# Three of eight weight pairs by seven products in the last projection's second half, with its row sums, a split affine step and a later halving of the last bank

## The chip, the cores and the metric

The kernel runs on one core of one Trainium2 chip. The metric is the device time of one execution in microseconds, the median over runs. A profile of one execution comes with it.

## The reference

The reference is one hybrid decoder layer on 256 tokens of width 2048, in float32: an input projection, two attention branches, a merge and an output projection with a layer norm, a gated MLP (width 5632) with a second layer norm, and a per-layer embedding at the end. What the change touches is the last line:

```python
x = layer_norm(ALPHA * x + ffn, ln2_g[i], ln2_b[i])
x = x + jax.nn.sigmoid(x @ w_ple_gate[i]) * (p[i] @ w_ple_proj[i])
```

The product x @ w_ple_gate is 256 x 2048 by 2048 x 2048. It is the last matrix product of the kernel, and everything that follows it is exposed.

## The kernel before, in words

**Splitting.** TensorE multiplies in a rounded float32 format (F32R). To keep the precision, each operand is split into a high part and a low remainder, and a product is the sum of three: high x high, high x low, low x high. Weights come in 284 units of 128 x 2048 floats. For each, SP issues two loads of 512 KB into `raw` (four buffers), ScalarE copies each into `hi` (line 231), and VectorE subtracts to get `lo` (line 236). `hi` and `lo` have six buffers each, which hold three units. The function `prep` (line 210) does that, and `unit` (line 254) calls it for a unit two or three places ahead of the one that TensorE takes.

**Plain pairs.** In the stages that compute token-major outputs, `x_half` (line 395) goes through the contraction in pairs of 128-row steps; a unit holds the weights of one pair for 1024 output columns. Two token halves (t) and two halves of the columns (c) make four PSUM banks of 512 columns. `x_mm` (line 340, its matmul on line 353) issues, for each of the two steps of a pair, 2 token halves x 3 products x 2 column halves: 24 matmuls of 512 columns a pair.

**Pairs by seven products.** A pair is also a 2 x 2 block product (two token halves, two contraction steps), and Strassen's scheme with seven products in place of eight does it with 21 matmuls (`seven`, line 356, its matmuls on line 373). It needs combinations of the weights (`combine_all`, line 144, computes them early on VectorE, lines 149 and 152, and stores them in DRAM as `tfd`, line 154), which `prep_seven` (line 161) later loads as `full` and splits into `ts` (line 179). It also needs sums of the activations (`x_sums`, line 376), split in the same way. Three of the seven products go straight into three of the four banks; the other four gather in four extra banks `ms`, and behind the last such pair a function `joined` adds those on VectorE into the four outputs. The gv, wo and dn stages work so for some of their pairs. The list of pairs is GVW, WOW or DNW.

**The last stage.** The gate product is done in two halves of 1024 columns, pg0 and pg1 (units 268 to 275 and 276 to 283), of eight pairs each. pg0 starts beside the second layer norm; pg1 keeps its last two pairs as a tail (`tail=2`), which is gone through bank by bank, so that the evacuation of one bank runs beside the matmuls of the next. With `fine=True` pg1's last bank (t = 1, c = 1) is kept in two halves of 256 columns, `pg1_11` and `pg1_11b`, for the whole of its sum, so that the very last evacuation is short. The evacuation `ev_o` (lines 1539 to 1551) is tanh on ScalarE (line 1545), two operations on VectorE (1546, 1548) and a store.

**What runs beside it.** The generator `affine` (line 1182, its operation on line 1187) multiplies the normalized `z2` by the gain and adds the bias, in sixteen steps of 128 x 512 on VectorE. `pull(n)` takes n steps of such generators behind each pair; in pg0 it is three a pair.

**What sets the order.** The queue of SP, which issues the loads, is in program order. The other engines' orders are chosen by a scheduler that places what is ready, the earlier in the program first. `keep_in_program_order` pins an instruction behind the one written last before it on the same engine; each step of `affine` is pinned so. The pool S8 has 15 tiles of 128 x 2048 floats: in the gate/up loop (`for n in range(NF)`, line 1371) it holds the four tiles of x1T, up to ten of hT, and the tiles of combinations.

Of the kernel before, what the change touches and what calls it, by code (L numbers as in the profile page):

```python
# [9 lines left out]
F32 = mybir.dt.float32  # L10
# [38 lines left out]
GV0 = 32  # L49
GVW = (1, 2, 4, 5)  # L50
WOW = ((1, 2, 4, 5), ())
WOP = tuple(sorted(set(WOW[0] + WOW[1])))
COMBW = range(14, 23)
COMB0 = 13
# [12 lines left out]
def tile_block(ctx: ExitStack, tc: tile.TileContext, wu, xw, wfv, wpp, xT_in, x_in, pT_in, wlr,  # L67
# [70 lines left out]
    tsi = {u: j for j, u in enumerate(units7)}  # L138
    tsd = dr.tile([len(units7), P, 1024], F32, name="tsd")
    units7w = [GV0 + i for i in GVW] + [WO0 + nh * 8 + i for nh in range(2) for i in WOW[nh]]  # L140
    tsw = {u: j for j, u in enumerate(units7w)}
    tfd = dr.tile([len(units7w), P, 2048], F32, name="tfd")

# [12 lines left out]
    def combs_gen(us):  # L156
        for u in us:
            yield from combine_all(u)
            yield
# [94 lines left out]
    def unit(ahead=3):  # L254
        u = n_used[0]
        n_used[0] += 1
        while n_prep[0] < min(NU, u + ahead):
            prep()
        return ready.pop(u)
# [77 lines left out]
        else:  # L337
            nc.vector.scalar_tensor_tensor(o, a, scale, tmp, ALU.mult, ALU.add)

    def x_mm(banks, w, a, toks, first, last, cs=(0, 1), part=None):  # L340


        hi, lo = w
        for t in toks:
            ah = a[:, t * P:t * P + P]
            al = a[:, 256 + t * P:256 + t * P + P]
            for i, (x, v) in enumerate(((ah, hi), (ah, lo), (al, hi))):
                for c in cs:
                    bs = banks[t][c]
                    m = 512 // len(bs)  # L350
                    for j in range(len(bs)) if part is None else (part,):
                        o = c * 512 + j * m
                        nc.tensor.matmul(bs[j][:, 0:m], lhsT=x, rhs=v[:, o:o + m],  # L353
                                         start=first and i == 0, stop=last and i == 2)

    def seven(banks, ms, w, act, kt, first, last):

# [35 lines left out]
                    mixers.pop(0)  # L393

    def x_half(name, act, K, evac, pulls=0, head=0, tail=0, mid=None, done=None, end=None,
               fine=False, ws=(), joined=None, begin=None, lean=False):


        ms = []
        banks = [[[mmtile(f"{name}_{t}{c}")] for c in range(2)] for t in range(2)]  # L400
        if fine:
            banks[1][1].append(mxtile(f"{name}_11b"))
        n = K // 2

        def mm(i, w, toks, cs=(0, 1), part=None):
            for j in range(2):
                kt = 2 * i + j
                x_mm(banks, (w[0][j], w[1][j]), act[kt // 4][:, kt % 4, :], toks,
                     kt == 0, kt == K - 1, cs, part)

        us = [unit(2) for _ in range(head)]
        if begin is not None:
            begin(lambda i, t: mm(i, us[i], (t,)))
        for i in range(head, n - tail):
            if i in ws:
                if i == ws[0]:
                    ms.extend(mmtile(f"{name}m{j}") if j % 2 == 0 else mxtile(f"{name}m{j}")
                              for j in range(4))
                seven(banks, ms, unit(), act, 2 * i, i == ws[0], i == ws[-1])
                if i == ws[-1]:  # L420
                    joined(ms)
            else:
                mm(i, unit(), (0, 1))
            pull(pulls)
            if mid is not None and i in mid:
                mid[i]()
        us = [unit(3 - (i if lean else 0)) for i in range(tail)]

        def tail_mm(t, c, i, put=True):
            mm(n - tail + i, us[i], (t,), (c,))  # L430
            if not put:
                return lambda: evac(t, c, banks[t][c][0])
            if i == tail - 1:
                evac(t, c, banks[t][c][0])

        if end is not None:
            end(tail_mm)
            return
        for t in range(2):
            for c in range(2):  # L440
                bs = banks[t][c]
                for j, ps in enumerate(bs):
                    for i, w in enumerate(us):
                        mm(n - tail + i, w, (t,), (c,), j)
                    if len(bs) == 1:
                        evac(t, c, ps)
                    else:
                        evac(t, c, ps[:, 0:256], (256 * j, 256 * j + 256))
            if done is not None:
                done(t)  # L450
# [502 lines left out]
    mixers.append(o_gen())  # L953


    combw = combs_gen(units7w[len(GVW):])


    sg = [s8([P, 8, 256], name=f"sg{i}") for i in range(4)]
# [411 lines left out]
    for n in range(NF):  # L1371
        if COMB0 <= n < COMB0 + len(units7):
            combs.append(combine(units7[n - COMB0]))
        for c in list(combs):
            if next(c, 1) == 1:
                combs.remove(c)
        if n % 4 == 0:
            hT[n // 4] = (s8 if n < 40 else lt)([P, 4, 512], F32R, name=f"hT{n // 4}")
        psg = gate_up(f"psg{n}")
        g = gp[n % 2]  # L1380
        comb(psg, g[:, 2:258])
        cw = [chn[:, c_cw + j * NF + n:c_cw + j * NF + n + 1] for j in range(3)]
        for i in range(2):
            nc.gpsimd.tensor_copy(g[:, 258 + i:259 + i], g[:, 129 - i:130 - i])
        y = t1("yc")
        nc.vector.tensor_scalar(y, g[:, 2:258], cw[2], chn[:, c_cb + n:c_cb + n + 1],
                                ALU.mult, ALU.add)
        y3 = y.rearrange("p (b n) -> p b n", b=2)
        for j, o in ((1, 1), (0, 0)):
            tap = g[:, o:o + 264 - 4 * o].rearrange("p (b n) -> p b n", b=2)[:, :, 0:P]  # L1390
            nc.vector.scalar_tensor_tensor(y3, tap, cw[j], y3, ALU.mult, ALU.add)
        nc.scalar.activation(y, y, AF.Gelu_apprx_tanh, bias=0.0, scale=1.0)
        psu = gate_up(f"psu{n}")
        u = t1("up")
        comb(psu, u)
        nc.vector.tensor_tensor(y, y, u, ALU.mult)
        dst = hT[n // 4][:, n % 4, :]
        copy(dst[:, 0:256], y)
        nc.vector.tensor_tensor(dst[:, 256:512], y, dst[:, 0:256].bitcast(F32), ALU.subtract)
        if n % 2 == 1 and n // 2 in DNP:  # L1400
            sf = t2("hs")
            x_sums(before[0], y, sf)
            for i, nm in enumerate(("hsh", "hsl")):
                sp = sm.tile([P, 512], F32R, tag="t2", bufs=6, name=nm)
                if i == 0:
                    sh = sp
                    copy(sp, sf)
                else:
                    nc.vector.tensor_tensor(sp, sf, sh.bitcast(F32), ALU.subtract)
                nc.gpsimd.dma_start(hsd[DNP.index(n // 2), :, i, :], sp.bitcast(F32))  # L1410
        before[0] = y
        if n >= 4:
            pull(1)
# [113 lines left out]
        border.close()  # L1527

    residual("dn", hT, NF, z2, st2, ({16: lambda: mid2(0), 17: lambda: mid2(1)}, {8: mid2a, NF // 2 - 5: mid2b}), end=end2, ws=DNW)
    mixers.append(affine(z2, gain[1], lambda t: None))  # L1530

    def mid3():
        for t in range(2):
            nc.sync.dma_start(pp[0][:, t, :], ppd[t])

    for nh in range(2):
        def ev_o(t, c, ps, ab=(0, 512), nh=nh):
            th = t2("tho")  # L1540
            r = t2("res")
            e = slice(*ab)
            w = slice(c * 512 + ab[0], c * 512 + ab[1])
            o = slice(nh * 1024 + w.start, nh * 1024 + w.stop)
            nc.scalar.activation(th[:, e], ps, AF.Tanh, bias=0.0, scale=0.5)
            nc.vector.scalar_tensor_tensor(th[:, e], th[:, e], 1.0, pp[nh][:, t, w],
                                           ALU.add, ALU.mult)
            nc.vector.scalar_tensor_tensor(r[:, e], th[:, e], 0.5, z2[t][:, o],
                                           ALU.mult, ALU.add)
            q = nc.gpsimd if nh == 0 else nc.sync  # L1550
            q.dma_start(out[t, :, o], r[:, e])
        x_half(f"pg{nh}", x2T, 16, ev_o, pulls=3, head=2 if nh == 0 else 0,
               tail=2 if nh == 1 else 0, mid={4: mid3} if nh == 0 else None,
               fine=nh == 1, begin=begin3 if nh == 0 else None)
    assert n_used[0] == NU, (n_used[0], NU)


# [33 lines left out]
def _layout(i):  # L1591
# [4 lines left out]
    for n in range(16):  # L1596
        br.append(bg[n:n + 1])
        if n % 2 == 0:
# [4 lines left out]
         _wst(c("gk", 1024)), _swap(_xst(c("gv", 2048)), GVW), _xst(c("gr", 2048)),  # L1603
         _wst(c("ma", 2048)), _wst(c("mb", 2048))] + br
        + [_swap(_xst(i["w_out"][0]), [h * 8 + p for h in range(2) for p in WOW[h]]), gu, _swap(_xst(i["w_down"][0]), [h * (NF // 2) + p for h in range(2) for p in DNW[h]]),
           _xst(i["w_ple_gate"][0])], 0)
    wfv = np.concatenate([c("fv", 1024), c("glr", 16), c("ff", 8)], 1)
    wfv = wfv.reshape(8, 2, P, NS)
    x = _fold(i["x"][0])
# [44 lines left out]
```

## Time and profile before

| | |
|---|---|
| median of three runs | 1649.1 us (1648.88 to 1650.4) |
| the profiled execution, its own time | 1649.94 us |
| its span, first to last instruction | 1648.1 us |
| TensorE matmuls (PE) | 1641.7 us busy, 8944 instructions |
| TensorE weight loads (PEld) | 1425.0 us |
| VectorE (DVE) | 1257.7 us, 1867 instructions |
| ScalarE (ACT) | 889.2 us |
| GpSimd (POOL) | 107.5 us |
| HBM read, written | 375.85 MB, 33.56 MB |

Busy times are shares of one span of 1648.1 us. Matmuls overlap, so a busy PE says that matmuls stood in line, not how fast they went: the pace is read from the chain that ended last, where each piece of work stands with its start, its length and how many instructions it took. A line such as "L353" is a line of the kernel; "pg<-hi,x2T" names what an instruction writes and reads, with the buffers' numbers left out. The time ahead of an instruction in which its engine sat idle stands in brackets, with what ended it.

### The profile page before, as it was taken

To read this page: it belongs to the slowest core of one execution; us is meant where nothing else is said; L and a number is where in the kernel's file an instruction comes from. 1 tells how busy PE (TensorE), PEld (TensorE's weight loads), DVE (VectorE), ACT (ScalarE), POOL (GpSimd) and SP (SyncE) were. 2 spreads that over 40 slices of the span, in tenths; PEclk is the share of its full clock that TensorE was granted. 3 is DMA by queue.
4 is the path that set the end of the run, shared out by engine and by line. 5 is a ranking of instruction groups with operands and counts; after the bars stand their busy time and mean duration, and the time that the engine had idled before them with its cause. 6 is when DMAs were issued, how large, how long until landed. Compare 5 with 4: busy or idle time off the path is not lost.

```text
span 1648.1 us, 24437 instructions
## 1 busy us (share of the span) xinstructions
PE 1641.7 (100%) x8944; PEld 1425.0 (86%) x8944; DVE 1257.7 (76%) x1867; ACT 889.2 (54%) x1277; POOL 107.5 (7%) x243
## 2 busy tenths in 40 slices
PE   9999999999999999999999999999999999999998
PEld 8988888888888888888898888888888888888887
DVE  6667667868876757786888778888877687888884
ACT  6745555545555555555565545555555565466652
POOL 0000000000000010000010011111110011010000
PEclk9999999999999999999999999999999999999999
DMA  7667787555556776668747678888876588899363
GB/s 298 232 233 278 260 268 256 180 185 179 178 175 241 258 235 238 197 206 318 268 150 236 232 261 310 346 326 333 325 284 221 189 299 302 286 331 355 149 235 123
DMA packets 110855, 411.01 MB, mean 249 GB/s; under 512 B 13016, under 2 KB 13920, under 8 KB 106256
## 3 DMA queue, kind: packets, MB, share of 16 engines
q1 hardware_dynamic: 98160, 359.96, 62.8%
q0 software_dynamic: 12432, 49.30, 7.8%
q8 instruction: 70, 1.15, 0.3%
q14 instruction: 49, 0.40, 0.1%
q10 hardware_dynamic: 144, 0.20, 0.0%
HBM read 375.85 MB, written 33.56 MB: 248 GB/s over the span
## 4 chain that ended last, share of the span: by engine, by line
PE 97%; DMA 1%; DVE 1%; ACT 0%; issue 0%; SPq 0%; ACTq 0%; DVEq 0%
PE psu L309 9%; PE psg L309 9%; PE psm L309 7%; PE dn L353 7%; PE gr L353 5%; PE pg L353 5%; PE psu L311 5%; PE psg L311 5%; PE gv L353 4%; PE wo L353 4%; PE psm L311 4%; PE psa L309 4%; PE fv L515 3%; PE dn L373 2%; PE psfk L309 2%; PE psq L309 2%
## 5 line engine op out<-in xcount | busy, mean ns | idle before, releaser
L236 DVE TENSOR_TENSOR lo<-raw,hi 128x1024 fp32r<-128x1024 f32 x494 | 601.3, 1226 | 206.7 <-ACT hi L231 205.2
L231 ACT ACTIVATE hi<-raw 128x1024 fp32r<-128x1024 f32 x494 | 519.1, 1058 | 397.2 <-DMA raw<-in_wu_dram 124.7
L309 PE MATMUL psu<-x1T,hi 128*128 128x512 f32 x688 | 236.0, 389 | 0.0
L309 PE MATMUL psg<-x1T,hi 128*128 128x512 f32 x672 | 230.5, 389 | 0.0
L311 PE MATMUL psu<-x1T,lo 128*128 128x256 f32 x688 | 189.9, 276 | 0.0
L311 PE MATMUL psg<-x1T,lo 128*128 128x256 f32 x672 | 185.5, 276 | 0.0
L309 PE MATMUL psm<-xT,hi 128*128 128x512 f32 x512 | 176.0, 391 | 0.0
L309 PEld LDWEIGHTS psu<-x1T,hi 128*128 128x128 f32 x688 | 129.1, 188 | 26.8
L309 PEld LDWEIGHTS psg<-x1T,hi 128*128 128x128 f32 x672 | 126.2, 188 | 26.3
L311 PE MATMUL psm<-xT,lo 128*128 128x256 f32 x512 | 141.5, 276 | 0.0
L311 PEld LDWEIGHTS psu<-x1T,lo 128*128 128x128 f32 x688 | 129.1, 188 | 0.0
L311 PEld LDWEIGHTS psg<-x1T,lo 128*128 128x128 f32 x672 | 126.2, 188 | 0.0
L309 PEld LDWEIGHTS psm<-xT,hi 128*128 128x128 f32 x512 | 96.1, 188 | 19.8
L353 PE MATMUL dn<-hi,hT 128*128 128x512 f32 x352 | 97.8, 389 | 0.0
L311 PEld LDWEIGHTS psm<-xT,lo 128*128 128x128 f32 x512 | 96.2, 188 | 0.2
L309 PE MATMUL psa<-oT,hi 128*128 128x512 f32 x256 | 87.8, 389 | 0.0
L353 PEld LDWEIGHTS dn<-hi,hT 128*128 128x128 f32 x352 | 66.0, 188 | 13.7
L311 PE MATMUL psa<-oT,lo 128*128 128x256 f32 x256 | 70.7, 276 | 0.0
L353 PE MATMUL gr<-hi,xT 128*128 128x512 f32 x256 | 70.6, 392 | 0.0
L353 PE MATMUL pg<-hi,x2T 128*128 128x512 f32 (+1 forms) x224 | 60.0, 376 | 0.0
L309 PEld LDWEIGHTS psa<-oT,hi 128*128 128x128 f32 x256 | 48.1, 188 | 10.1
L353 PEld LDWEIGHTS gr<-hi,xT 128*128 128x128 f32 x256 | 47.5, 188 | 9.4
(386 smaller groups left out, 3159.0 us busy)
## 6 DMA issues: line engine op xcount, KB each, us to landing
raw<-in_wu_dram SPq DMA_DIRECT2D x524, 512.0 KB, 5.2
comb<-in_wu_dram SPq DMA_DIRECT2D x22, 768.0 KB, 8.4
tsd<-comb POOLq DMA_DIRECT2D x22, 512.0 KB, 7.4
top<-tsd SPq DMA_DIRECT2D x22, 512.0 KB, 6.4
combw<-in_wu_dram SPq DMA_DIRECT2D x8, 1024.0 KB, 8.1
tfd<-combw POOLq DMA_DIRECT2D x8, 1024.0 KB, 5.2
full<-tfd SPq DMA_DIRECT2D x8, 1024.0 KB, 8.3
fvraw<-in_wfv_dram SPq DMA_DIRECT2D x15, 524.0 KB, 8.1
```

The lines of the kernel that those rows point to most:

```text
L231: c = nc.scalar.activation(hi, raw, AF.Copy, bias=0.0, scale=1.0)
L236: return nc.vector.tensor_tensor(lo, raw, hi.bitcast(F32), ALU.subtract)
L309: nc.tensor.matmul(ps, lhsT=hi[i // 8 if hoff == 0 else 0][:, w0 % 1024:w0 % 1024 + P], rhs=a[:, kt % 4, :], start=first and i == 0, stop= ...
L311: nc.tensor.matmul(ps[:, 256:512], lhsT=lo[i // 8 if hoff == 0 else 0][:, w0 % 1024:w0 % 1024 + P], rhs=a[:, kt % 4, 0:256], start=False, ...
L353: nc.tensor.matmul(bs[j][:, 0:m], lhsT=x, rhs=v[:, o:o + m], start=first and i == 0, stop=last and i == 2)
L373: nc.tensor.matmul(ps, lhsT=a, rhs=v, start=m and first and i == 0, stop=m and last and i == 2)
L515: nc.tensor.matmul(fbk[t][c][:, 0:n], lhsT=x, rhs=w[:, o:o + n], start=kt == 0 and i == 0, stop=kt == 15 and i == 2)
```

## The change

Pairs 1, 3 and 4 of pg1 are done by seven products. That takes six edits:

- the weights' combinations of these three units are computed in the gate/up loop, begun at n = 35, 37 and 39; on the host their four column blocks are put in the order that the scheme wants;
- the sums of the activations are made from the split activations (high + low on VectorE, four sums, then a copy on ScalarE and a subtraction), in three generators `p_sums(j)` for j = 0, 1, 2 (pairs 1, 3, 4);
- the affine step is made in halves: first the columns of pg0's output, then p_sums(0) and p_sums(1), then the columns of pg1's output, then p_sums(2). Two steps are pulled behind each pair of pg0 and four behind each of pg1;
- behind pair 4, `joined_p` adds the four extra banks into `pj`, and each evacuation of pg1 adds its part of `pj` on VectorE before the tanh;
- the last bank is one bank of 512 columns up to the tail; it is closed behind pair 5 and added into `pj` (`last_p`), and two new half banks are opened for the tail alone;
- the pulls are 2 and 4 in place of 3 and 3.

```diff
+PG1 = 276
+PGW = (1, 3, 4)
...
     units7w = [GV0 + i for i in GVW] + [WO0 + nh * 8 + i for nh in range(2) for i in WOW[nh]]
+    units7w += [PG1 + i for i in PGW]
...
-                                         start=first and i == 0, stop=last and i == 2)
+                                         start=(first or again and t == c == 1) and i == 0,
+                                         stop=(last or shut and t == c == 1) and i == 2)
...
-        if fine:
+        if fine and not ws:
             banks[1][1].append(mxtile(f"{name}_11b"))
         n = K // 2
+        shut = max((i for i in range(n - tail) if i not in ws), default=-1) if fine and ws else -1
...
+        if shut >= 0:
+            fine(banks[1][1][0])
+            banks[1][1] = [mmtile(f"{name}_11a"), mxtile(f"{name}_11b")]
         us = [unit(3 - (i if lean else 0)) for i in range(tail)]
...
     for n in range(NF):
         if COMB0 <= n < COMB0 + len(units7):
             combs.append(combine(units7[n - COMB0]))
+        j = n - COMB0 - len(units7)
+        if j in range(0, 2 * len(PGW), 2):
+            combs.append(combine_all(PG1 + PGW[j // 2]))
...
-    mixers.append(affine(z2, gain[1], lambda t: None))
+    def p_sums(j):
+        a = x2T[PGW[j] // 2]
+        e = slice(2 * PGW[j] % 4, 2 * PGW[j] % 4 + 2)
+        sh, sl = sums[PG1 + PGW[j]]
+        both, sf = t2("psb").rearrange("p (k t) -> p k t", t=S), t2("psf")
+        tc.keep_in_program_order(nc.vector.tensor_tensor(
+            both, a[:, e, 0:256].bitcast(F32), a[:, e, 256:512].bitcast(F32), ALU.add))
+        yield
+        x_sums(both[:, 0, :], both[:, 1, :], sf)
+        yield
+        copy(sh, sf)
+        nc.vector.tensor_tensor(sl, sf, sh.bitcast(F32), ALU.subtract)
+        yield
+
+    def for_gate():
+        yield from affine(z2, gain[1], lambda t: None, (0, 1))
+        yield from p_sums(0)
+        yield from p_sums(1)
+        yield from affine(z2, gain[1], lambda t: None, (2, 3))
+        for j in range(2, len(PGW)):
+            yield from p_sums(j)
+
+    mixers.append(for_gate())
...
+    def joined_p(ms):
+        p1, p5, p7, p6 = ms
+        j = s8([P, 4, 512], name="pj")
+        pj.extend(j[:, i, :] for i in range(4))
+        u = t2("ju")
+        copy(pj[0], p1)
+        for o, a, p in ((u, pj[0], p6), (pj[1], u, p5), (pj[2], u, p7), (pj[3], pj[2], p5)):
+            nc.vector.tensor_tensor(o, a, p, ALU.add)
+
+    def last_p(ps):
+        nc.vector.tensor_tensor(pj[3], pj[3], ps, ALU.add)
...
+            if pj:
+                nc.vector.tensor_tensor(th[:, e], ps, pj[2 * t + c][:, e], ALU.add)
+                ps = th[:, e]
             nc.scalar.activation(th[:, e], ps, AF.Tanh, bias=0.0, scale=0.5)
...
-        x_half(f"pg{nh}", x2T, 16, ev_o, pulls=3, head=2 if nh == 0 else 0,
+        x_half(f"pg{nh}", x2T, 16, ev_o, pulls=2 + 2 * nh, head=2 if nh == 0 else 0,
                tail=2 if nh == 1 else 0, mid={4: mid3} if nh == 0 else None,
-               fine=nh == 1, begin=begin3 if nh == 0 else None)
+               fine=last_p if nh == 1 else None, ws=PGW if nh == 1 else (), joined=joined_p,
+               begin=begin3 if nh == 0 else None)
...
-           _xst(i["w_ple_gate"][0])], 0)
+           _swap(_xst(i["w_ple_gate"][0]), [8 + p for p in PGW])], 0)
```

More of the change, by code (lines that the diff above doesn't have):

```diff
@@ L338, in comb, with x_mm @@
             nc.vector.scalar_tensor_tensor(o, a, scale, tmp, ALU.mult, ALU.add)
-    def x_mm(banks, w, a, toks, first, last, cs=(0, 1), part=None):
+    def x_mm(banks, w, a, toks, first, last, cs=(0, 1), part=None, shut=False,
+             again=False):
         hi, lo = w
@@ L395, in x_half @@
     def x_half(name, act, K, evac, pulls=0, head=0, tail=0, mid=None, done=None, end=None,
-               fine=False, ws=(), joined=None, begin=None, lean=False):
+               fine=None, ws=(), joined=None, begin=None, lean=False):
         ms = []
         banks = [[[mmtile(f"{name}_{t}{c}")] for c in range(2)] for t in range(2)]
-        if fine:
+        if fine and not ws:
             banks[1][1].append(mxtile(f"{name}_11b"))
         n = K // 2
+        shut = max((i for i in range(n - tail) if i not in ws), default=-1) if fine and ws else -1
         def mm(i, w, toks, cs=(0, 1), part=None):
@@ L408, in mm @@
                 x_mm(banks, (w[0][j], w[1][j]), act[kt // 4][:, kt % 4, :], toks,
-                     kt == 0, kt == K - 1, cs, part)
+                     kt == 0, kt == K - 1, cs, part, j == 1 and i == shut,
+                     j == 0 and shut >= 0 and i == n - tail)
         us = [unit(2) for _ in range(head)]
@@ L953, in tile_block @@
     mixers.append(o_gen())
-    combw = combs_gen(units7w[len(GVW):])
+    combw = combs_gen(units7w[len(GVW):-len(PGW)])
     sg = [s8([P, 8, 256], name=f"sg{i}") for i in range(4)]
@@ L1529, in tile_block @@
     residual("dn", hT, NF, z2, st2, ({16: lambda: mid2(0), 17: lambda: mid2(1)}, {8: mid2a, NF // 2 - 5: mid2b}), end=end2, ws=DNW)
-    mixers.append(affine(z2, gain[1], lambda t: None))
+    psums = [lt([P, 2, 2, 512], F32R, "hT10"), s8([P, 2, 2, 512], F32R, name="ps1")]
+    for j, i in enumerate(PGW):
+        sums[PG1 + i] = psums[j // 2][:, j % 2, 0, :], psums[j // 2][:, j % 2, 1, :]
+    def p_sums(j):
[19 more added lines that the diff above has]
+    mixers.append(for_gate())
     def mid3():
@@ L1536, in mid3 @@
             nc.sync.dma_start(pp[0][:, t, :], ppd[t])
+    pj = []
+    def joined_p(ms):
[8 more added lines that the diff above has]
+        nc.vector.tensor_tensor(pj[3], pj[3], ps, ALU.add)
     for nh in range(2):
```

## The prediction

> **What bounds the kernel now.** I read the page first (busy times, the chain that ended last), then the chain of waits in two stages, then busy time by stretch of the last 80 us, then the order on VectorE there.
>
> ```profile
> PE 1641.7 (100%) x8944; PEld 1425.0 (86%) x8944; DVE 1257.7 (76%) x1867; ACT 889.2 (54%) x1277; POOL 107.5 (7%) x243
> PE 97%; DMA 1%; DVE 1%; ACT 0%; issue 0%; SPq 0%; ACTq 0%; DVEq 0%
> ```
>
> TensorE is the bound: the chain is 97% PE, so a matmul removed anywhere is time removed, as long as its operands are ready. The chain in the first GLA value half (gv0) gives the price of both kinds of pair, start, us, what:
>
> ```profile
> 243.73 5.46 PE gv L353 x24
> 249.20 1.36 PE gv L373 x6
> ...
> 258.72 5.44 PE gv L353 x24
> ```
>
> A plain pair (24 matmuls of 512 columns) takes 5.44 to 5.46 us. From 249.20 to 258.72 lie two pairs by seven products, 42 matmuls: 4.76 us each. The chain in the stage that the change edits:
>
> ```profile
> 1564.99 35.99 PE pg L353 x159
> 1600.98 0.12 PE pg_11b L353
> ...
> 1606.56 0.12 PE pg_11b L353
> ...
> 1632.71 8.19 PE pg L353 x36
> 1640.92 0.61 ACT tho L1545
> 1641.55 0.70 DVE tho L1546
> 1642.27 0.53 DVE res L1548
> ...
> 1642.88 0.43 DVE tho L1546
> ...
> 1643.34 0.43 DVE res L1548
> ...
> 1643.79 0.39 ACT tho L1545
> ...
> 1644.20 0.44 DVE tho L1546
> ...
> 1644.66 0.42 DVE res L1548
> ```
>
> In pg0 a pair costs 24 x 35.99/159 = 5.43 us. In pg1 the last bank is two half banks through the whole sum, and the same point of the next pair comes 1606.56 - 1600.98 = 5.58 us later. So pg1's six pairs ahead of its tail take 33.5 us and begin at 1632.71 - 33.5 = 1599.2. Behind the matmuls only the evacuations of the last banks remain.
>
> **What the change removes on TensorE.** Pairs 1, 3 and 4 become 21 matmuls, 0, 2 and 5 become undivided: 3 x 4.76 + 3 x 5.44 = 30.6 us, 2.9 us less. The half banks' share of that: 6 x (5.58 - 5.44) = 0.8 us, half of it on the pairs that stay plain. This is the whole gain, and no other row offers more.
> A rule speaks against the smaller part: the Trainium skill, TensorE: Matmul & The Clock Gate, section "Wait — 56ns, not 53.3ns?", puts the fixed cost of one more warm matmul at 2.5 ns, which would make 36 divided matmuls cost 0.09 us and the gain 3 x (5.44 - 4.76) + 0.09 = 2.1 us. The trace has 0.14 us a pair, and the trace decides.
>
> **What it adds at the end.** Each evacuation of pg1 gets an addition on VectorE ahead of the tanh. Nearest rows, with others that the sum needs (group, count | busy, mean ns):
>
> ```profile
> L1147 DVE TENSOR_TENSOR z<-z,dn 128x512 f32<-128x512 f32 x8 | 5.3, 683 | 2.0 <-PE dn L353 2.0
> L1546 DVE SCALAR_TENSOR_TENSOR tho<-tho,ppk 128x256 f32<-128x256 f32 x2 | 0.8, 422 | 0.4 <-ACT tho L1545 0.4
> L179 DVE TENSOR_TENSOR ts<-full,ts 128x1024 fp32r<-128x1024 f32 x16 | 19.1, 1220 | 15.0 <-ACT ts L118 15.0
> L179 DVE TENSOR_TENSOR lo<-rawl,hi 128x512 fp32r<-128x512 f32 x8 | 5.5, 687 | 0.9 <-ACT hi L118 0.9
> L382 DVE TENSOR_TENSOR hs<-yc 128x128 f32<-128x128 f32 x24 | 6.9, 289 | 0.6
> L149 DVE TENSOR_TENSOR combw<-combw 128x512 f32<-128x512 f32 x16 | 11.0, 686 | 7.9 <-DMA combw<-in_wu_dram 7.7
> L152 DVE TENSOR_TENSOR combw<-combw 128x1024 f32<-128x1024 f32 x8 | 9.8, 1222 | 0.2
> ```
>
> Whole banks: 0.68 us on VectorE against 2.72 us of matmuls (8.19/3), hidden but for the last. Lower bound: the final half bank's addition alone, 0.42. Upper bound: the addition of the last whole bank (second token half, first column half) and both halves' (0.68 + 0.42 + 0.42), if VectorE takes the evacuations strictly one after another, plus a second tanh of 0.39 that no longer runs beside them: 1.9. The scheduler places what is ready, so I take 1.0.
>
> **What it adds on VectorE ahead of pair 4: the term that decides.** Busy time in stretches of the last stage (length; busy us and instructions of PE, PEld, DVE, ACT, POOL; granted clock; DMA share; GB/s), and VectorE's own order there:
>
> ```profile
> 1585.00:1598.00 13.00, 13.00 (x60) 10.74 (x59) 11.38 (x13) 5.59 (x6) 0.00 (x0) 1.00 0.74 241
> 1598.00:1604.00 6.00, 6.00 (x32) 5.08 (x31) 5.50 (x9) 4.86 (x7) 1.68 (x3) 1.00 0.52 195
> 1604.00:1612.00 8.00, 8.00 (x45) 6.89 (x44) 4.37 (x5) 2.12 (x2) 0.54 (x1) 1.00 0.90 270
> 1612.00:1630.00 18.00, 18.00 (x101) 15.52 (x100) 9.74 (x8) 7.43 (x7) 0.00 (x0) 1.00 0.43 141
> ```
>
> ```profile
> 1573.37 2.01 DVE L1187 TENSOR_TENSOR z<-z,lnb 128x512 f32<-128x512 f32 x3
> ...
> 1598.36 0.69 DVE L1546 SCALAR_TENSOR_TENSOR tho<-tho,ppk 128x512 f32<-128x512 f32 x1 [1.56 <-ACT tho L1545]
> ...
> 1603.68 4.62 DVE L236 TENSOR_TENSOR lo<-raw,hi 128x1024 fp32r<-128x1024 f32 x4
> ```
>
> VectorE is nearly full to 1604 and then half idle. The change moves eight affine steps into that idle part and adds work beside them. The row sums of pair 4 (p_sums(2)) stand behind all of it in the code: line by line, the first step is pinned behind the last affine step, that behind the split of pair 4's weights, and four affine steps behind the split of pair 3's. From 1598.36, when pg0's evacuations begin, VectorE has to do: those evacuations, 1603.68 - 1598.36 = 5.3; pair 2's plain split, 2 x 1.15 (4.62/4) = 2.3; the splits of pairs 3 and 4, 0.6 + 3 x 1.15 = 4.0 each, 8.0 (512 columns take 0.69 alone and some 0.6 in a row of others, as 1024 take 1.22 and 1.15); eight affine steps, 8 x 0.66 (2.01/3) = 5.3; the rest of p_sums(1), four sums of 0.29 and a subtraction of 0.6 = 1.8; p_sums(2), 0.66 + 1.2 + a copy on ScalarE and a subtraction of about 0.6 each (the tanh of 512 columns took 0.61) = 3.1. That is 25.8 us: done at 1624.2. TensorE, unhindered, reaches pair 4 at 1599.2 + 5.44 + 4.76 + 5.44 + 4.76 = 1619.6, and its first product reads those sums. A wait of 4.6 us. Below that: if p_sums(1) and two affine steps (3.1 us) get done in the gap before 1598.36, 1.5. Above: pair 1's split spills over (up to 2.3: it reads 1.75 MB in place of 1, with the DMA engines 0.74 busy already) and pair 5's slips in ahead (up to 2.3): 9.2. In the stretch 1585 to 1598 only 1.6 us are free on VectorE, so little is done early and some spill is likely: I take 5.0, near the plain count. Nothing hides it; all matmuls of pg1 stand behind pair 4 in TensorE's queue. The other additions cost nothing: p_sums(0) and p_sums(1) are read by pairs 1 and 3, 5.4 and 15.6 us into pg1; joined_p (a copy, four additions of 0.68) and the closing of the last bank (one addition) have the tail's 8.19 us before the two half banks open; ScalarE, with 1.5 copies more a pair, is busy 5.59 of 13.00 us; the four extra banks are the two that pg0 frees at its evacuation and the two of the layer norm's turn, done before. If that cover went, each would add about its own length, under 1 us.
>
> **What it adds in the gate/up loop.** Three combinations (n = 35, 37, 39): 3 x (2 x 0.69 + 1.22) = 7.8 us of VectorE, three loads on SP between the weights' loads, three stores on POOL. From n = 36 ten hT and four x1T tiles hold 14 of 15 S8 buffers, so the second and third load wait on SP for the store before, and all weights behind them wait too.
>
> ```profile
> 1223.00:1289.00 66.00, 66.00 (x390) 58.37 (x389) 49.86 (x74) 35.47 (x52) 3.31 (x14) 1.00 0.69 232
> 1307.00:1320.00 13.00, 13.00 (x78) 11.47 (x78) 9.22 (x16) 6.47 (x10) 2.86 (x7) 1.00 0.45 160
> ```
>
> ```profile
> 1307.26 0.33 SPq L172 DMA_DIRECT2D raw<-in_wu_dram  x1
> 1319.93 0.33 SPq L173 DMA_DIRECT2D top<-tsd  x1
> tfd<-combw POOLq DMA_DIRECT2D x8, 1024.0 KB, 5.2
> ```
>
> VectorE has 66 - 49.9 = 16 us free there. And SP already stands 12.7 us for such a buffer at 1307 while PE stays full (13.00 of 13.00): that is the cover. Lower bound 0, upper 5.2 (one store beyond the cover); I take 0.3, near the row.
>
> **Sum.** -2.9 + 1.0 + 5.0 + 0.3 = +3.4 us. The profiled execution took 1649.94 us (span 1648.1 and 1.8 around it) and would take 1653.3; the median of the three runs is 0.8 lower, so I forecast 1652.5. A measurement tells about 0.2% (3.3 us) from no change, and this lies at that line, on the slow side.
>
> **Rivals.** *The sums come in time* (the other side). If the scheduler fills VectorE so that p_sums(2) waits under 3 us, which holds from the point where its 25.8 us shrink to 24 or less, the gain shows: with a wait of 0 to 3 us, 1649.1 - 2.9 + 1.0 + 0.3 + 0 to 3 = 1647.5 to 1650.5, no change that can be told. For it: the 9.74 busy of 18.00 us behind 1612, and ops that are ready do jump the queue. Against it: the pins. Faster by over 3.3 us it cannot be, since -2.9 + 0.4 is the most.
> *The wait also drops TensorE's clock.* All rows so far show it at 1.00, but:
>
> ```profile
> 1.19 3.59 PE L130 MATMUL warm_ps<-warm 128*128 128x512 bf16 x8 [1.19 <-DVE warm L127]
> 1643.80:1646.00 2.20, 0.00 (x0) 0.00 (x0) 0.85 (x2) 0.37 (x1) 0.00 (x0) 1.00 0.49 183
> 1646.00:1648.00 2.00, 0.00 (x0) 0.00 (x0) 0.00 (x0) 0.00 (x0) 0.00 (x0) 0.89 0.18 61
> ```
>
> After the last matmul the mean falls to 0.89 in two microseconds: if full and half clock are mixed, half since about 1647.6, 3.8 us after PE went idle. At the start eight matmuls take 3.59 us, 0.45 each against 0.227 in pg0. So a wait over some 3.8 us may cost as much again: if 4 us of work then run at half rate, 2 us more, 1654.5. The Trainium skill, same page, section "What's actually happening", makes it a free-running window of 3.4 us that must be wholly idle; by that, a wait of 5.0 us would trip it in about half of the cases.
> *SP's waits in gate/up come through*: up to +5.2 with a wait at pair 4 under 3, about 1652.5.
>
> **How the numbers follow.** Wait at pair 4, clock holds: 0.33 (its own range 1650.8 to 1656.7, a wait of 3.3 to 9.2). Sums in time: 0.40. Clock drops: 0.20. Gate/up: 0.07. Of the first case a third stays under 3.3 us over the median, of the last half. Slower: 0.22 + 0.20 + 0.04 = 0.46; faster 0.02, for chance alone; same 0.52. A wait at pair 4, with or without the clock, has 0.53 and sets the time, at its likeliest length with the clock held; time and chances lie close to the 0.2% line. The range goes from 1647.0 (no wait, the tail near its lower bound) to 1656.5 (the clock variant with a longer wait).
>
> **What would show it.** Right: pg1's plain pairs at 5.44 and sevens at 4.76 in the chain; an idle stretch of TensorE before the first seven-product matmul of pair 4, released by the subtraction of p_sums on VectorE; full VectorE from 1598 to about 1625; SP standing at combw loads with TensorE full. Wrong: pair 4 starting without a gap, a stall at pair 1 or 3, or gaps in the gate/up loop.

## The result and the profile after

The changed kernel takes 1652.3 us, the median of 19 runs (1650.02 to 1653.78). The kernel before, run beside it, takes 1649.1 (19 runs, 1648.24 to 1650.4). The ratio is 1.0017, with a 95% interval of 1.001 to 1.0024. That is 3.1 us more: under the line of 0.2% that the prediction set for a change that can be told, though the interval leaves 1 out. The forecast was 1652.5. The profiled execution is among the fastest: 1650.32 us with a span of 1648.5, 0.4 over that of before. One execution of tail_light, a variant below, ran at a granted clock of 0.75 and took 2049.8 us; it is not among the runs counted here.

The stretches that the prediction showed for before (length; busy us and instructions of PE, PEld, DVE, ACT, POOL; clock; DMA share; GB/s), now of the changed kernel:

```profile
1585.00:1598.00 13.00, 13.00 (x60) 10.74 (x59) 11.54 (x17) 7.51 (x10) 0.00 (x0) 1.00 0.71 260
1598.00:1604.00 6.00, 6.00 (x28) 4.99 (x27) 5.86 (x10) 3.61 (x5) 1.84 (x4) 1.00 0.94 310
1604.00:1612.00 8.00, 8.00 (x37) 6.64 (x36) 7.34 (x13) 4.36 (x6) 0.38 (x1) 1.00 0.92 323
1612.00:1630.00 18.00, 17.02 (x72) 13.02 (x72) 17.01 (x24) 9.74 (x11) 0.00 (x0) 1.00 0.50 177
```

Behind 1598 VectorE was busy 5.50 + 4.37 + 9.74 = 19.6 of 32 us; now it is 5.86 + 7.34 + 17.01 = 30.2 of 32. And TensorE, full before, has lost about 1 us of the last stretch. VectorE's order there, from the first evacuation of pg0 to the last step of pair 4's sums (start, length, instruction, idle time ahead and what ended it):

```profile
1598.14 0.69 DVE L1603 SCALAR_TENSOR_TENSOR tho<-tho,ppk 128x512 f32<-128x512 f32 x1
...
1606.47 0.49 DVE L387 TENSOR_TENSOR psf<-psb 128x128 f32<-128x128 f32 x2 [0.66 <-DMA out_dram<-res]
...
1620.12 1.22 DVE L239 TENSOR_TENSOR lo<-raw,hi 128x1024 fp32r<-128x1024 f32 x1
...
1621.86 0.68 DVE L1553 TENSOR_TENSOR psb<-x2T 128x512 f32<-128x512 f32 x1
1622.46 1.22 DVE L239 TENSOR_TENSOR lo<-raw,hi 128x1024 fp32r<-128x1024 f32 x1
...
1625.31 0.69 DVE L1559 TENSOR_TENSOR ps<-psf,ps 128x512 fp32r<-128x512 f32 x1 [0.69 <-ACT ps L120]
```

The queue is 1626.00 - 1598.14 = 27.9 us long, not 25.8. The sums of pair 4 are the last thing in it, and two splits of pair 5's weights (L239) stand ahead of them. TensorE at the same time:

```profile
1618.62 0.39 PE L378 MATMUL pg<-hi,x2T 128*128 128x512 f32 x1
...
1619.98 0.84 PE L378 MATMUL pg<-ts,x2T 128*128 128x512 f32 x3
1620.66 0.39 PE L357 MATMUL pg<-hi,x2T 128*128 128x512 f32 x1
1621.39 0.50 PE L357 MATMUL pg<-lo,x2T 128*128 128x512 f32 x1 [0.34 <-DVE lo L239]
...
1624.07 0.62 PE L357 MATMUL pg<-hi,x2T 128*128 128x512 f32 x2
1625.33 0.50 PE L378 MATMUL pg<-hi,ps 128*128 128x512 f32 x1 [0.63 <-ACT ps L120]
```

Pair 4 begins at 1618.62, but with the nine of its 21 matmuls that read x2T and no sums (L378, to 1620.66). Behind them stand 13 matmuls of pair 5 (L357), which the scheduler has put in front of the rest of pair 4. Only then comes the wait for `ps`. The sums came 6.7 us after the pair was begun, and 22 matmuls at 0.227, 5.0 us, lay in between. So little more than 1.7 us was lost. By the rows, half of that (0.9 us) is the wait for `ps`; the other half lies in pair 5, which waits for the low parts of its own weights (`lo`, L239), from the same queue of VectorE. Without these waits TensorE would have come to `ps` earlier and stood there longer, as the sums come last.

The end, in the chain that ended last (start, us, what):

```profile
1633.64 0.70 DVE tho L1600
...
1636.45 0.62 DVE tho L1600
...
1639.17 0.61 DVE tho L1600
...
1641.94 0.35 DVE tho L1600
...
1643.64 0.35 DVE tho L1600
1644.01 0.42 ACT tho L1602
...
1644.91 0.42 DVE res L1605
```

Five additions (L1600), one for each whole bank and each half bank, 2.8, 2.7, 2.8 and 1.7 us apart, and all of it VectorE and the tanh that it waits for. In before this chain was TensorE's until 1640.92. From the first addition to the last result it is 1645.33 - 1633.64 = 11.7 us.

### The profile page after: what moved, and what is told of

Read it like the earlier page. It is cut to its first block, busy times and chain, and to the rows that moved or that the text cites. A ratio compares the mean times of both kernels' runs of the same rounds, so it can differ in the third digit from the quotient of the medians.

```text
span 1648.5 us, 24409 instructions
## 1 busy us (share of the span) xinstructions
PE 1639.3 (99%) x8899; PEld 1422.0 (86%) x8899; DVE 1278.7 (78%) x1910; ACT 894.7 (54%) x1287; POOL 115.2 (7%) x246
## 4 chain that ended last, share of the span: by engine, by line
PE 90%; issue 4%; DVE 2%; DMA 2%; ACT 1%; POOL 0%; SPq 0%; ACTq 0%; DVEq 0%; POOLq 0%
PE psu L312 9%; PE psg L312 9%; PE psm L312 7%; PE dn L357 6%; PE gr L357 5%; PE psu L314 5%; PE psg L314 5%; PE gv L357 4%; PE wo L357 4%; PE psm L314 4%; PE psa L312 4%; PE fv L525 3%; PE dn L378 2%; PE psq L312 2%; PE psfk L312 2%
## 5 line engine op out<-in xcount | busy, mean ns | idle before, releaser
L239 DVE TENSOR_TENSOR lo<-raw,hi 128x1024 fp32r<-128x1024 f32 x488 | 591.9, 1222 | 194.0 <-ACT hi L234 190.6
L234 ACT ACTIVATE hi<-raw 128x1024 fp32r<-128x1024 f32 x488 | 511.3, 1057 | 358.8 <-DMA raw<-in_wu_dram 117.9
L357 PE MATMUL dn<-hi,hT 128*128 128x512 f32 x352 | 97.8, 389 | 0.0
L357 PEld LDWEIGHTS dn<-hi,hT 128*128 128x128 f32 x352 | 66.0, 188 | 13.7
L357 PE MATMUL gr<-hi,xT 128*128 128x512 f32 x256 | 70.6, 392 | 0.0
L357 PEld LDWEIGHTS gr<-hi,xT 128*128 128x128 f32 x256 | 47.5, 188 | 9.4
L357 PE MATMUL dn<-lo,hT 128*128 128x512 f32 x176 | 55.5, 389 | 0.0
```

Of the source, the lines that this page charges most:

```text
L234: c = nc.scalar.activation(hi, raw, AF.Copy, bias=0.0, scale=1.0)
L239: return nc.vector.tensor_tensor(lo, raw, hi.bitcast(F32), ALU.subtract)
L357: nc.tensor.matmul(bs[j][:, 0:m], lhsT=x, rhs=v[:, o:o + m], start=(first or again and t == c == 1) and i == 0, stop=(last or shut and t = ...
```

## The experiments

Three numbers were taken from every trace. *Stage*: from the start of the first matmul that writes a pg bank to the end of the last one. *Gaps*: what the starts of neighbouring matmuls of the stage lie apart beyond the pace of 0.227 us, where they are over 0.26 apart (the first 20 us of the stage, with the layer norm in them, left out). *Behind*: from the end of the last matmul to the end of the last `res`.

| kernel | median, us (runs) | ratio to before, 95% | stage | gaps | behind |
|---|---|---|---|---|---|
| before | 1649.1 (19) | | 89.8 | 0 | 1.3 |
| after | 1652.3 (19) | 1.0017, 1.001 to 1.0024 | 88.9 | 1.8 | 3.4 |
| after_again | 1652.9 (8) | 1.0026, 1.0016 to 1.0035 | 90.7 | 3.7 | 3.4 |
| after_third | 1652.4 (1) | | 90.3 | 3.2 | 3.4 |
| before_plus_add | 1651.7 (12) | 1.0024, 1.001 to 1.0039 | 89.8 | 0 | 3.4 |
| before_plus_combs | 1649.2 (11) | 1.0002, 0.9993 to 1.0011 | 89.8 | 0 | 1.3 |
| sums_early | 1651.1 (11) | 1.0013, 1.0005 to 1.0022 | 88.1 | 1.0 | 4.8 |
| pulls_more | 1652.7 (11) | 1.002, 1.0011 to 1.0028 | 88.1 | 1.1 | 4.6 |
| tail_light | 1651.6 (10) | 1.0014, 1.0005 to 1.0023 | 91.0 | 3.9 | 2.3 |
| affine_pool | 1660.8 (5) | 1.0069, 1.0057 to 1.0082 | 99.8 | 12.7 | 3.4 |
| both_light | 1659.8 (5) | 1.0067, 1.0054 to 1.0079 | 97.9 | 10.8 | 2.3 |
| early_light | 1649.3 (11) | 0.9998, 0.9989 to 1.0007 | 89.1 | 1.9 | 2.3 |
| two_pairs | 1649.2 (11) | 0.9997, 0.9988 to 1.0006 | 87.6 | 0 | 3.4 |
| two_light | 1647.7 (11) | 0.9989, 0.998 to 0.9998 | 87.7 | 0 | 2.3 |

Theory A: the change loses its gain to VectorE, once as a wait for the sums at pair 4 and once as additions at the end. The rivals put the loss elsewhere: the end alone, the gate/up loop, the clock.

**after_again** and **after_third**: the changed kernel, unaltered.

> The changed kernel once more, unaltered. Its first profile had TensorE idle some 2.0 us around pair 4 of the last half, and 3.4 us from the last matmul to the last result where before it was 1.3; against the matmuls' 2.9 us that makes about +1 over before, but the medians differ by 3.1. Theory A (the wait at pair 4 is longer in a typical execution than in the profiled one): this profile shows either more than 2 us of gaps around pair 4, or the same gaps and a time near 1650.5. Theory B (something outside the last stage differs between executions, the clock for instance): gaps around pair 4 are again 2.0 +- 0.3, and a time that is 2 us longer shows it elsewhere in the trace. Median under both: 1652.3 +- 0.6.

> The changed kernel a third time, one look. Its first profile lost 1.8 us at pair 4 with the clock held, its second 3.7, of which the clock's fall for 3.4 us is 1.7. Theory A (VectorE's queue is 27.9 to 28.3 us long from the first evacuation of the first half on, and that begins 45.1 to 46.8 us into the stage, as the loads let it): the subtraction of p_sums(2) ends 28.1 +- 0.4 us behind the first evacuation again, and the loss at pair 4 is the later of that against TensorE, 1.8 to 4 us, more if a window of the clock falls into the gaps. Rival: the queue's length itself varies, and the loss does not follow the first evacuation.

The third execution bears theory A out. Its first evacuation of pg0 and its last step of pair 4's sums:

```profile
1599.63 0.68 DVE L1603 SCALAR_TENSOR_TENSOR tho<-tho,ppk 128x512 f32<-128x512 f32 x1
...
1627.38 0.69 DVE L1559 TENSOR_TENSOR ps<-psf,ps 128x512 fp32r<-128x512 f32 x1 [0.69 <-ACT ps L120]
```

Again 28.4 us (28.3 in the second). The queue's length holds; its start moves from 45.1 us into the stage (first profile) to 46.2 and 45.9, and the loss at pair 4 goes with it, from 1.8 to 3.7 and 3.2. So the first profile showed a short wait. What TensorE stood for one after the other in the third:

```profile
1621.73 0.73 PE L378 MATMUL pg<-ts,x2T 128*128 128x512 f32 x2 [0.72 <-DVE ts L182]
...
1623.47 0.50 PE L357 MATMUL pg<-lo,x2T 128*128 128x512 f32 x1 [0.78 <-DVE lo L239]
...
1627.40 0.50 PE L378 MATMUL pg<-hi,ps 128*128 128x512 f32 x1 [0.63 <-ACT ps L120]
```

First the split of pair 4's own weight combinations (`ts`), then pair 5's `lo`, then the sums: all three come out of VectorE's queue, and the sums last. In the second a fall of the clock lay in the gaps:

```profile
1615.70:1619.12 3.42, 3.42 (x17) 2.81 (x15) 3.42 (x5) 2.40 (x3) 0.00 (x0) 1.00 0.64 216
1619.12:1622.53 3.41, 1.83 (x7) 0.93 (x6) 3.41 (x5) 0.00 (x0) 0.00 (x0) 1.00 0.35 112
1622.53:1625.94 3.41, 3.41 (x10) 2.66 (x9) 2.69 (x7) 0.65 (x2) 0.00 (x0) 0.50 0.60 187
1625.94:1629.36 3.42, 3.42 (x16) 2.82 (x16) 3.15 (x4) 3.42 (x5) 0.00 (x0) 1.00 0.34 120
```

The cuts at 1622.53 and 1625.94 are where the clock changed, the others whole steps of 3.41 us from there. After 3.41 us with 7 matmuls in place of 17 the granted clock is 0.50 for just as long. It cost little: the half-rate matmuls are those of pair 5, which only filled the time until the sums came. The loss is 3.7 us with the clock's fall and 3.2 without, one execution each, with the sums ready 74.5 and 74.4 us into the stage.

**before_plus_add**: the addition at the end, alone.

```diff
+    zj = lt([P, 512], F32, "zj")
+    nc.vector.memset(zj, 0.0)
...
+            if nh == 1:
+                nc.vector.tensor_tensor(th[:, e], ps, zj[:, e], ALU.add)
+                ps = th[:, e]
```

> The kernel before, with one thing of the change: an addition on VectorE ahead of each tanh of the second half, here of a bank of zeros (one memset more, the order of all else as before). The prediction took 1.0 us for it, from the addition of the last half bank and part of the others. The trace of the changed kernel has 2.1 us more from the last matmul to the last result. If that is the addition's own price with VectorE taking bank after bank: before +2.1, last matmul to last result 3.4 us. If part of the 2.1 comes from what else the change put there (the closing of the split bank, the order of the tail): before +1.0, about 2.3 us.

```profile
1633.85 0.69 DVE L1549 TENSOR_TENSOR tho<-pg,zj 128x512 f32<-128x512 f32 x1 [5.99 <-PE pg L353]
1635.24 0.69 DVE L1552 SCALAR_TENSOR_TENSOR tho<-tho,ppk 128x512 f32<-128x512 f32 x1 [0.70 <-ACT tho L1551]
1635.97 0.69 DVE L1554 SCALAR_TENSOR_TENSOR res<-tho,z 128x512 f32<-128x512 f32 x1
1636.58 0.69 DVE L1549 TENSOR_TENSOR tho<-pg,zj 128x512 f32<-128x512 f32 x1
...
1642.02 0.41 DVE L1549 TENSOR_TENSOR tho<-pg,zj 128x256 f32<-128x256 f32 x1
...
1643.71 0.42 DVE L1549 TENSOR_TENSOR tho<-pg_11b,zj 128x256 f32<-128x256 f32 x1
...
1645.07 0.42 DVE L1554 SCALAR_TENSOR_TENSOR res<-tho,z 128x256 f32<-128x256 f32 x1
```

The addition alone puts 3.4 us behind the last matmul in place of 1.3, so it is its own price, all 2.1 us of it. The rows tell why. A bank takes VectorE three operations and 0.70 us of standing idle for the tanh, 1636.58 - 1633.85 = 2.73 us. The matmuls of a bank took 8.19/3 = 2.73. VectorE goes at exactly TensorE's pace and makes up nothing. It comes to the first half bank at 1642.02, when the last matmul of both halves is about to end (1642.12), so that both halves are still to be done, one after another, 1.7 us each.

**sums_early** and **pulls_more**: two ways to have pair 4's sums earlier.

```diff
         yield from p_sums(1)
-        yield from affine(z2, gain[1], lambda t: None, (2, 3))
         for j in range(2, len(PGW)):
             yield from p_sums(j)
+        yield from affine(z2, gain[1], lambda t: None, (2, 3))
```

```diff
-        x_half(f"pg{nh}", x2T, 16, ev_o, pulls=2 + 2 * nh, head=2 if nh == 0 else 0,
+        x_half(f"pg{nh}", x2T, 16, ev_o, pulls=3 + nh, head=2 if nh == 0 else 0,
```

> The sums of pair 4 are computed ahead of the last eight affine steps, nothing else is changed. Theory A (pair 4 waits for its sums behind VectorE's queue): no gap over 0.35 us on TensorE between pairs 3 and 5, and at least 2.0 us less than the changed kernel, up to 4 if the wait of typical executions is what separates the medians: 1648.3 to 1650.3. Rival (the time is lost at the end, in the evacuations, and elsewhere outside pair 4): 1652 as the changed kernel, within 0.7.

> Three steps a pair in the first half and four in the second, where the changed kernel has two and four: the sums of pairs 1 and 3 come before the first half's evacuations, and do not wait for a buffer that the stores of these evacuations hold (0.66 us of an empty VectorE in the profile). Theory A: p_sums(2) ends 3 us or more earlier, the gaps at pair 4 shrink under 0.5 us, 2 to 4 us less than the changed kernel. A variant (A2: the landing of the store decides how long the wait of an execution is): the same, and the spread of the runs falls from 3.8 us to 2 or less. Rival (the end alone): within 0.7 of the changed kernel.

In sums_early the wait at pair 4 is gone, as theory A has it, but only 1.2 to 1.7 us of the runs' time with it (against the two medians of the changed kernel), less than the 2.0 expected. Its end shows where the rest stayed:

```profile
1631.08 1.22 DVE L239 TENSOR_TENSOR lo<-raw,hi 128x1024 fp32r<-128x1024 f32 x1
1632.22 0.68 DVE L1587 TENSOR_TENSOR pj<-pj,pg1m 128x512 f32<-128x512 f32 x1
1633.00 0.69 DVE L1590 TENSOR_TENSOR pj<-pj,pg 128x512 f32<-128x512 f32 x1
1633.60 0.68 DVE L1600 TENSOR_TENSOR tho<-pg,pj 128x512 f32<-128x512 f32 x1
1634.98 0.69 DVE L1603 SCALAR_TENSOR_TENSOR tho<-tho,ppk 128x512 f32<-128x512 f32 x1 [0.70 <-ACT tho L1602]
```

There is no idle time in front of the first addition: VectorE has the displaced affine steps, the splits and the joining to do until 1633.60, and from there its 11.7 us run. TensorE's stage was 0.8 us shorter, with 1.0 us of gaps close to its end, and 4.8 us were left behind it. Most of the wait had only moved to the end. In pulls_more too the stage is shorter and the end longer. Its profile still loses 1.1 us at pair 4, where under 0.5 was expected; and its runs are as slow as the changed kernel's and as wide apart (3.6 us), so the part of theory A that put the spread down to the landing of a store (A2) fell. By its time alone pulls_more came out as the rival (the end alone) has it. That its median lies 2 us above what its one profile adds up to is not explained.

**before_plus_combs**: the combinations in the gate/up loop, alone.

```diff
+    units7w += [276 + i for i in (1, 3, 4)]
...
+        j = n - COMB0 - len(units7)
+        if j in range(0, 6, 2):
+            combs.append(combine_all(276 + (1, 3, 4)[j // 2]))
```

> The kernel before, with the three combinations for the last stage added in the gate/up loop and nothing else: their results are stored and not used. It also gives a second profile of the kernel before in the last stage. The prediction took 0.3 us for this term, between 0 and 5.2; the trace of the changed kernel has no gap over 0.35 us on TensorE there. Theory (SP's waits have TensorE's cover): before +0 to 0.3 us. Rival (what the medians show beyond the profiles' sums, some 1 to 2 us, sits in this loop in typical executions): before +1 or more.

```profile
1223.00:1289.00 66.00, 66.00 (x389) 58.34 (x389) 52.48 (x79) 33.46 (x50) 8.95 (x15) 1.00 0.85 307
```

VectorE is 2.6 us busier there than before, TensorE full, and the time the same: the rival fell, and this term is nothing.

**tail_light**: less on VectorE at the end. The `put` of begin3 scales pp[1] by 0.5, and:

```diff
+                    v = nc.vector if half else nc.gpsimd
+                    keep(v.tensor_tensor(r[:, e], th[:, e], z2[t][:, o], ALU.add))
...
+            held.append(rest)
+            if not half or ab[0]:
+                while held:
+                    held.pop(0)()
```

> The changed kernel with less on VectorE behind the last matmuls: the last addition of each whole bank of the second half goes to GpSimd (with the factor 0.5 already in the projection), and the two half banks' additions of the joined products are placed ahead of the first half's two other steps. Theory A (the end of the kernel is VectorE's, which takes bank after bank with 0.7 us idle for each tanh): last matmul to last result falls from 3.42 to about 2.1 us, and the median by about 1.3. Rival (GpSimd's additions slow VectorE down or take over 2.7 us each): no gain, or up to 1 us slower than the changed kernel.

```profile
1643.22 0.42 DVE L1604 TENSOR_TENSOR tho<-pg_11b,pj 128x256 f32<-128x256 f32 x1 [0.40 <-PE pg_11b L357]
...
1645.02 0.42 DVE L1616 TENSOR_TENSOR res<-tho,z 128x256 f32<-128x256 f32 x1
```

VectorE now waits for the last half bank's matmuls (PE), and 2.3 us remain behind them. Behind the last matmul that is 1.2 us less, and the median gained 0.6 to 1.2 (against the two medians of the changed kernel). The gaps at pair 4 were 3.9 us in this trace, more than in any of the changed kernel.

**affine_pool** and **both_light**: the second eight affine steps on GpSimd (`nc.gpsimd.tensor_tensor` in place of `nc.vector.tensor_tensor`); both_light has the light tail as well.

> The changed kernel with the second eight affine steps on GpSimd in place of VectorE. It takes 5.4 us from VectorE's queue ahead of the sums of pair 4. Theory A (VectorE's queue makes TensorE wait at pair 4): no gap there, the stretch from the first matmul of the stage to the last falls from 88.9 to about 86.9 us (the full 2.9 under before), and VectorE is ready at the tail, so that 3.4 us remain behind the last matmul, not 4.6 to 4.8 as where only the order was changed. Median 2 us or more under the changed kernel: 1650.5 or lower. Rival (the lost time is not the queue's length): same as with the sums ahead, 1651.1, or slower, if the two engines slow each other down.

> Both of the other two: the second affine steps on GpSimd and the light tail. Theory A, additive: 88.9 - 2.0 us for the stage's matmuls and 2.1 behind them; against before (89.8 and 1.3) that is 2.1 us less, 1646.9. If GpSimd's two kinds of work collide or its additions are long, the gain is one of the two alone, 1649 to 1650.5.

The rival came true, and far beyond its price. Groups of affine_pool between 1605 and 1621 (busy, mean ns), and TensorE at pair 4:

```profile
L387 DVE TENSOR_TENSOR psf<-psb 128x128 f32<-128x128 f32 x2 | 2.7, 1382 | 0.0
L1197 POOL TENSOR_TENSOR z<-z,lnb 128x512 f32<-128x512 f32 x8 | 14.2, 1789 | 0.3
```

```profile
1629.27 0.80 PE L378 MATMUL pg<-hi,ps 128*128 128x512 f32 x1 [5.94 <-ACT ps L120]
```

A sum of 128 x 128 that takes VectorE 0.29 us took 1.38 beside GpSimd's additions. The queue got longer (31.0 us from the first evacuation to the end of the sums), and TensorE stood 5.9 us at pair 4, at half clock behind it. Here only three matmuls of the pair, and none of pair 5, stood ahead of the sums, so that little hid the wait. So the test went the wrong way round, but it shows the same link: what is added to VectorE ahead of the sums is lost on TensorE. In both_light the light tail took its part off the end (2.3 us), and the gaps (10.8 us) outweighed it.

**early_light**, **two_pairs**, **two_light**: the edits of sums_early and tail_light together; only pairs 1 and 3 by seven products; and those with the light tail.

```diff
-PGW = (1, 3, 4)
+PGW = (1, 3)
...
-    psums = [lt([P, 2, 2, 512], F32R, "hT10"), s8([P, 2, 2, 512], F32R, name="ps1")]
+    psums = [lt([P, 2, 2, 512], F32R, "hT10")]
```

> The sums of pair 4 ahead of the affine steps, and the light tail, nothing on GpSimd but the three last additions of the tail. Theory A (VectorE's queue sets both the wait at pair 4 and the start of the tail): the stage's matmuls 88.1 us as with the sums ahead alone, VectorE comes to the tail 1.3 us late but takes 2.1 us a bank in place of 2.7 and catches up, 2.2 us from last matmul to last result: 90.3 against 91.2 in the profile of before, so 1648.1 us, 0 to 1 under before. Rival (gains of the two do not add, since VectorE is late by as much as the tail saves): 1650.5 to 1651.

> Only pairs 1 and 3 by seven products, so that pair 4 needs no sums and VectorE some 5 us less, with the light tail. TensorE loses one pair's 0.68 us of the gain. Theory A: no gap at pair 4, stage 89.8 - 2.2 = 87.6 us, 2.2 behind it, 89.8 against 91.2: 1647.6 us, 1 to 2 under before. Rival (something else in the change costs 1 to 2 us in typical executions, whatever VectorE's load): 1649 or more.

> The changed kernel with pairs 1 and 3 by seven products and pair 4 plain, the tail as the change has it. No sums of pair 4, so no wait for them, while the additions of the evacuations stay. Theory A (the wait at pair 4 and the tail are the two prices, and they add): the stage 89.8 - 2.2 = 87.6 us without a gap, 3.4 us behind the last matmul, 91.0 to 91.1 against 91.2: the time of before within 0.5 us, some 3 us under the changed kernel. Rival (the third pair is no worse than the others, and the loss is spread over the change): 1651 or more.

Two_pairs is the clean test. Without the third pair the gaps are gone, the stage is 87.6 us as expected, and with the same tail the kernel takes as long as before (0.9997). So the third pair, which saves TensorE 0.68 us, made the runs some 3 us longer. Early_light is between its two forecasts, no faster than before: the gaps come back at other places (1.9 us), which fits a VectorE that is too full for all three pairs. Two_light is the fastest, 1.1 in a thousand under before (0.2 to 2.0), which is still within the prediction's 0.2%. The chain of its last stage:

```profile
1607.78 5.44 PE pg L357 x24
1613.22 1.36 PE pg L378 x6
1614.58 2.72 PE pg1m L378 x12
1617.30 0.68 PE pg L378 x3
1617.98 19.04 PE pg L357 x84
...
1641.73 0.43 DVE res L1616
```

A plain pair 5.44, a pair by seven 1617.98 - 1613.22 = 4.76, and no gap up to the last banks.

## Why the forecast held, and which of its steps did not

- **TensorE, -2.9 us: right.** Two pairs should have given 2.9 - 0.68 = 2.2: from 89.8 to 87.6 us in two_pairs. With three, 88.9 less 1.8 of gaps is 87.1, 2.7 under before. The half banks' share was real: with the 2.5 ns that the Trainium skill (TensorE: Matmul & The Clock Gate, section "Wait — 56ns, not 53.3ns?") has for one more matmul, two_pairs would have gained an estimated 2 x 0.68 + 0.09 = 1.45 us.
- **The tail, 1.0 us: mis-sized.** It is 2.1, beyond the upper bound of 1.9. The step took it that "whole banks" are "hidden but for the last". That needs VectorE to be faster than TensorE's 2.72 us a bank, and with the addition it takes 2.73.
- **The wait at pair 4, 5.0 us: the place right, the size wrong twice.** VectorE's queue was full to 1626 as said, and what TensorE waited for last was the sums (the copy on ScalarE, not yet the subtraction; in the second profile the slow clock brought it there after them). It reached pair 4 65.6 us into the stage, where the sum had 65.7. The sums came later than thought, 72.3 us and more into it in place of 70.3: pair 5's first two splits slipped in ahead, 0.66 us was lost to the buffer of a store, and the queue began later. By itself that was a wait of 6.7. But "nothing hides it; all matmuls of pg1 stand behind pair 4 in TensorE's queue" failed. Nine matmuls of the pair do not read the sums, and the scheduler had put 13 of pair 5 in front. Of the wait 1.8 to 3.2 us remained, 3.7 with the clock's fall. So the sign that the prediction named for being wrong, pair 4 starting without a gap, came true in all three profiles: the gaps stood inside the pair and in pair 5, while VectorE was full to 1626 as the other sign has it.
- **Gate/up, 0.3 us: nothing**, by its own kernel. The sign named for it, SP standing at combw loads, was not in the trace.
- **The sum.** -2.7 + 2.1 + 1.8 to 3.2 = +1.2 to +2.6 us; from the first matmul of the stage to the last result the first and the third profile are 1.2 and 2.5 longer than that of before, the second, with the clock's fall, 3.0, and the medians 3.1. That the forecast of +3.4 came out so near is luck: two errors met, the tail 1.1 too small and the wait 1.8 to 3.2 too long, and the medians lie above what two of the three profiles add up to.
- **The rivals.** *The sums come in time* did not happen in any of the three profiles. *The wait also drops the clock* happened in one, and cost some 0.5 us in place of 2, by that execution against the third, as the slow matmuls lay in the wait itself.

What stays open: the medians lie 1 to 2 us above the profiled executions in several of the kernels with the addition (after 2.0, after_again 1.6, pulls_more 1.9, before_plus_add 1.2, two_pairs 1.6), but not in before_plus_combs, early_light or two_light (0.3, -1.0 and 0.5). Before_plus_add and two_pairs have no gap at pair 4, so a wait there that is longer in other executions cannot be the whole of it. Profiles of the timed runs would be needed to say more.

## What to carry to other kernels

Before trading matmuls for additions, add up the other engine's work over the whole stretch to the end, the evacuations included: here the first two pairs paid for their additions (with the lighter tail a little more than that), and the third, with VectorE at 30 of 32 us, did not. That a bank's matmuls are longer than an operation added to its evacuation does not hide that operation: compare the whole cycle with its idle times, 2.73 against 2.73 us. And for the price of a wait, read from the order of the instructions what stands between the arrival and the first one that really needs the data.

## What was not expected of the hardware

Additions on GpSimd and VectorE held each other up. One on GpSimd at the end of tail_light, beside a VectorE addition that reads PSUM, and a VectorE sum of the changed kernel with GpSimd idle:

```profile
1637.08 1.28 POOL L1616 TENSOR_TENSOR res<-tho,z 128x512 f32<-128x512 f32 x1 [31.93 <-DVE tho L1609]
```

```profile
L387 DVE TENSOR_TENSOR psf<-psb 128x128 f32<-128x128 f32 x4 | 1.0, 287 | 0.7 <-DMA out_dram<-res 0.7
```

In affine_pool, with both operands of both engines in SBUF, it was 1.79 and 1.38 us. The Trainium skill, GPSIMD Engine Reference, section "1. Specifications", has the two engines share their SBUF interfaces, with contention for VectorE instructions that read two inputs there; the trace agrees, and gives the price: up to 1.1 us on a VectorE operation. That was the same on larger ones (128x512 0.69 to 1.76 us, 128x1024 1.22 to 2.30), and two of the ten operations beside GpSimd's additions took their usual time. Such operations look held up more than slowed down; that is not shown.

The clock fell in after_again after a window in which TensorE was far from idle: 1.83 of 3.41 us busy, 7 matmuls in place of 17. The clock's four changes in that trace, at 4.61, 1622.53, 1625.94 and 1646.42 us, lie 474, 1 and 6 steps of 3.413 us apart, so windows are counted in such steps from a change. In the changed kernel's first profile, with 2.97 and 3.07 us busy (13 and 15 matmuls), the clock held:

```profile
1618.06:1621.47 3.41, 3.07 (x15) 2.22 (x13) 3.41 (x5) 0.36 (x1) 0.00 (x0) 1.00 0.41 145
1624.88:1628.30 3.42, 2.97 (x13) 2.35 (x14) 2.74 (x3) 3.42 (x5) 0.00 (x0) 1.00 0.38 140
```

The prediction, after the Trainium skill (TensorE: Matmul & The Clock Gate, section "What's actually happening"), had taken it that the window must be idle throughout. Here 1.58 us without a matmul in the window, made up of gaps of which none was over 0.81, went with a fall, while tail_light kept its clock with 2.08 us busy in a window (1618.61 to 1622.02), so 1.33 without.
